# Spreading each cache block's running maximum over the partitions: a transpose of a zero-step column in place of an fp32 product

## The chip, the cores and the metric

The kernel runs on one core of one Trainium2 chip. The metric is the device time of one launch in microseconds (us); lower is better. The same program was run three times, and one more execution was taken with the hardware profiler.

## What is computed

One inference step (one layer) of a hybrid decoder, for a prompt of 1024 tokens and for 8 sequences of 8 sampled tokens each. A combined input projection feeds gated linear attention (GLA) and multi-head latent attention (MLA); an output projection, a gated MLP with a short convolution and a gated per-layer embedding follow. The change lies in the MLA of the sampled tokens. They attend to a paged cache of 8192 latents per sequence, page by page, with a running maximum:

```python
def body(carry, phys):                       # one page of 128 cached latents
    c, r = pool_ckv[phys], pool_krope[phys]
    k, v = latent_to_kv(c, r, w_kvup, g_kn)
    return combine(carry, block_stats(q, k, v, None)), None

# block_stats: s = q.k * scale; m = max(s); p = exp(s - m); l = sum(p); acc = p.v
# combine:     m = max(m1, m2), and both l and acc rescaled by exp(m1 - m), exp(m2 - m)
```

Any shift of the scores that is the same in numerator and denominator gives the same output.

## The kernel before

**The cache stream.** The 8192 cached positions of each of the 8 sequences are worked through in 8 blocks of 1024 positions, 64 blocks in all; the first block of a sequence also takes the 8 new tokens. A block passes through a pipeline written as a generator, `cache_stream`: `stage_load` gathers the pages, `pre`/`turn` transpose the latents (L522, tile `ctp`), `main` forms key sizes and raw scores (L139 to L141, tile `ks`, and ScalarE's squares, tile `csq`), `stage_b` makes the scores `sn` and each column's maximum over the tiles, `stage_c1` makes the running maximum and the exponentials, and `stage_pv` multiplies them with the latents (L645, tile `cpv`).

**The place of the change** is `stage_c1`. The 64 score columns are 8 heads by 8 tokens, and the partition axis holds positions. L616 transposes the column maxima `ml` (128 partitions by 128, each column twice), so that partition c of `mt` holds the maxima of column c; L620 or L622 on VectorE reduces them, together with the old maximum `mo`, to `m` (tile `bm`, 128 partitions by 1). L626 must subtract `m` from scores whose columns lie along the free axis, so `m` has to be turned from a column into a row that stands alike in all 128 partitions. L625 does that on TensorE: it reads `m[0:64]` with a step of zero 128 times (`broadcast_to([64, P])`) as the stationary operand and multiplies it with a 64 x 64 identity in fp32. L628 (exponential), L629 and L630 (the split of the result in two fp32r parts `phl`) follow.

**What sets the order.** Two generators are interleaved while the program is built: the cache stream and `dense`, which holds the prompt's projections, GLA and prompt attention; `PACE` says how much estimated dense work goes with a cache step. After `dense` ends, `fill` and `place` put units of the output projection (`wo_unit`, L1432 to L1436, tile `ps_dn`) between the remaining cache blocks. Within that, the framework's scheduler orders the instructions of each engine by estimated times of its own, so a different instruction at one place can move others, on every engine. Each engine then works its list in order, and a wait of its first instruction holds everything behind it. SP issues most loads and stores as a list of the same kind; its stores wait for the engine that makes the data, its loads for a free staging buffer (three of them, tag `stage`).

Names in the rows below: `ps_pj`, `ps_kv`, `ps_gv`, `ps_lt` are sums of prompt projections; `stage` the staging buffers for weights (`w_in`, `mla_w_qup`, `mla_w_kvup`); `lat` the prompt's latents, stored as `ckv_p` and `krope_p`; `wraw` the raw rows of the output projection's weights `w_o`; `h_...` the residual rows loaded from `x_prompt`; `pt_ol` (L675) the transpose of one sequence's finished output, 64 partitions high.

Of the kernel before, what the change touches and what calls it, by code (L numbers as in the profile page):

```python
# [18 lines left out]
P = 128  # L19
# [25 lines left out]
def step_kernel(ctx: ExitStack, tc: tile.TileContext, A):  # L45
    nc = tc.nc
    pe, act, dve, pool, sp = nc.tensor, nc.scalar, nc.vector, nc.gpsimd, nc.sync
# [4 lines left out]
    def ctile(shape, dt, name):  # L52
        return const.tile(shape, dt, name=name, tag=name)
# [3 lines left out]
    ident = ctile([P, P], F32, "ident")  # L57
# [134 lines left out]
    def pm(shape, name):  # L192
        return psM.tile(shape, F32, tag="m", name=name)
# [412 lines left out]
    def stage_c1(o):  # L606

        nt = o.nt
        sb = o.sn[:, :nt, :]
        mt = pm([P, 512], "mt")  # L610
        drain = o.n - NB * 8 + 3
        if drain == 1:
            fill(49 - z["units"])
        elif drain == 2:
            fill(2)
        pe.transpose(mt[:, 0:P], o.ml.rearrange("p a c -> p (a c)"), ident)  # L616
        m = cp.tile([P, 1], F32, tag="bm", name="bm", bufs=4)
        mo = state.get(o.b)
        if mo is None:
            dve.tensor_reduce(m, mt[:, 0:P], AX.X, ALU.max)  # L620
        else:
            dve.tensor_scalar(mt[:, 256:256 + P], mt[:, 0:P], mo, None, ALU.max, ALU.max, accum_out=m)  # L622
        if drain > 0:
            fill(1)
        pe.matmul(mt[:, P:P + 64], m[0:64].broadcast_to([64, P]), ident[0:64, 0:64], start=True, stop=True)  # L625
        dve.tensor_tensor(sb, sb, mt[:, P:P + 64].unsqueeze(1).broadcast_to([P, nt, 64]), ALU.subtract)  # L626
        phl = cp.tile([P, 9, P], F32R, tag="phl", name="phl", bufs=1)
        act.activation(sb, sb, AF.Exp)  # L628
        act.copy(phl[:, :nt, 0:64], sb)  # L629
        pool.tensor_tensor(phl[:, :nt, 64:128], sb, phl[:, :nt, 0:64].bitcast(F32), ALU.subtract)  # L630
        o.phl = phl
        o.t = None
        if mo is not None:
            o.t = cp.tile([P, 1], F32, tag="mb", name="mb", bufs=4)
            act.activation(o.t, m, AF.Exp, bias=mo, scale=-1.0)
        state[o.b] = m
# [41 lines left out]
    def cache_stream():  # L678
# [7 lines left out]
        for n in range(N + 2):  # L686
            z["block"] = n
            if n + 2 < N:
                blk[n + 2] = stage_load(*todo[n + 2], n + 2)
            if n < N:  # L690
                pre(blk, blk[n], 4)
                main(blk[n], 0)
            if 0 <= n - 2:
                stage_pv(blk[n - 2])
            if 0 <= n - 1 < N:
                stage_b(blk[n - 1])
            yield
            if n < N:
                if blk[n].nt == 9:
                    pre(blk, blk[n], 8)  # L700
                    main(blk[n], 4)
                    pre(blk, blk[n + 1], 0)
                    main(blk[n], 8)
                else:
                    if n + 1 < N:
                        pre(blk, blk[n + 1], 0)
                    main(blk[n], 4)
            if 0 <= n - 1 < N:
                stage_c1(blk[n - 1])
            if 0 <= n - 2:  # L710
                stage_c2(blk.pop(n - 2))
            yield
# [882 lines left out]
    def fill(n):  # L1595
        for _ in range(n):
            z["units"] += next(z["fill"], done) is None
# [658 lines left out]
```

## Time and profile before

| | |
|---|---|
| median of three runs | 2220.92 us (2215.85 to 2221.26) |
| the profiled execution | 2221.39 us, of which the span from first to last instruction is 2219.6 us |
| TensorE (PE) busy | 2134.6 us, 96% of the span |
| VectorE (DVE), ScalarE (ACT), GpSimd (POOL) busy | 1666.6, 1369.1 and 1227.5 us |
| mean granted TensorE clock | 0.984 |
| L625 | first at 116.8 us, last at 1326.0 us, 64 blocks |
| after the cache stream | from about 1330 us: MLP, embedding |

In rows of instructions the columns are: start in us, length in us, engine, line, operation, output tile and inputs, shape, count, and in brackets how long the engine was idle before it and who released it. Lengths of matmuls overlap, because they are pipelined: what a matmul costs its neighbours is read from start to start. PEld is the load of a stationary operand. In rows of windows the columns are the stretch, its length, busy time (and count) of PE, PEld, DVE, ACT and POOL, the granted clock, the DMA engines' busy share and GB/s.

### The profile page before, as it was taken

To read this page: it belongs to the slowest core of one execution; us is meant where nothing else is said; L and a number is where in the kernel's file an instruction comes from. 1 tells how busy PE (TensorE), PEld (TensorE's weight loads), DVE (VectorE), ACT (ScalarE), POOL (GpSimd) and SP (SyncE) were. 2 spreads that over 40 slices of the span, in tenths; PEclk is the share of its full clock that TensorE was granted. 3 is DMA by queue.
4 is the path that set the end of the run, shared out by engine and by line. 5 is a ranking of instruction groups with operands and counts; after the bars stand their busy time and mean duration, and the time that the engine had idled before them with its cause. 6 is when DMAs were issued, how large, how long until landed. Compare 5 with 4: busy or idle time off the path is not lost.

```text
span 2219.6 us, 38384 instructions
## 1 busy us (share of the span) xinstructions
PE 2134.6 (96%) x13460; PEld 1934.7 (87%) x13460; DVE 1666.6 (75%) x2551; ACT 1369.1 (62%) x3726; POOL 1227.5 (55%) x1330
## 2 busy tenths in 40 slices
PE   7999999999999999999999987999999999999999
PEld 6888978878888888887788876999999999888899
DVE  4775676467788888887888878888888886887642
ACT  5576766777778888887777766433333433534631
POOL 5675668576777777777445557666656562011100
PEclk9899999999999999999999998999999999999999
DMA  5343234412342222221521212322232325778321
GB/s 181 110 141 110 77 117 157 141 54 69 104 120 60 64 73 61 60 56 46 167 80 57 76 66 96 105 92 95 91 100 91 100 87 190 238 222 237 98 72 41
DMA packets 204418, 233.07 MB, mean 105 GB/s; under 512 B 42422, under 2 KB 146339, under 8 KB 204227
## 3 DMA queue, kind: packets, MB, share of 16 engines
q1 hardware_dynamic: 188259, 179.49, 25.8%
q0 software_dynamic: 14736, 46.67, 7.3%
q10 hardware_dynamic: 1232, 4.46, 0.5%
q8 instruction: 108, 1.77, 0.3%
q14 instruction: 83, 0.68, 0.1%
HBM read 188.00 MB, written 42.52 MB: 104 GB/s over the span
## 4 chain that ended last, share of the span: by engine, by line
PE 80%; DVE 7%; ACT 5%; DMA 4%; POOL 2%; issue 2%; SPq 0%; DVEq 0%; POOLq 0%; ACTq 0%
PE ps_gu L140 7%; PE ps_gu L141 7%; PE ps_gu L139 7%; PE ks L139 5%; PE ks L141 5%; PE ks L140 4%; PE ps_dn L141 3%; PE ps_dn L140 3%; PE ps_dn L139 3%; PE cpv L645 2%; PE ctp L522 2%; PE ps_lt L278 2%; PE ps_pj L139 2%; PE ps_pj L140 1%; PE ps_pj L141 1%
## 5 line engine op out<-in xcount | busy, mean ns | idle before, releaser
L560 ACT ACTIVATE csq<-ks 128x256 f32<-128x256 f32 x1040 | 392.2, 400 | 88.1 <-PE ks L141 78.0
L565 DVE TENSOR_REDUCE css<-csq 128x16 f32<-128x1024 f32 (+1 forms) x264 | 315.8, 1197 | 63.0 <-ACT csq L560 61.9
L115 ACT CAST wh<-st 128x512 fp32r<-128x512 f32 x176 | 108.4, 619 | 188.6 <-PE ps_gu L140 166.0
L139 PE MATMUL ks<-mv0h,cTh 128*128 128x320 f32 (+1 forms) x520 | 171.9, 333 | 6.9 <-ACT csq L560 3.0
L139 PE MATMUL ks<-mv1h,cTh 128*128 128x320 f32 (+1 forms) x520 | 170.4, 329 | 7.6 <-ACT sn L562 3.6
L604 POOL TENSOR_TENSOR chl<-craw,chl 128x1024 fp32r<-128x1024 f32 x64 | 141.8, 2216 | 57.9 <-ACT chl L603 57.2
L140 PE MATMUL ks<-mv1l,cTh 128*128 128x320 f32 (+1 forms) x520 | 154.0, 298 | 0.0
L140 PE MATMUL ks<-mv0l,cTh 128*128 128x320 f32 (+1 forms) x520 | 153.0, 296 | 0.0
L141 PE MATMUL ks<-mv0h,cTl 128*128 128x320 f32 (+1 forms) x520 | 148.6, 298 | 0.9 <-DVE cTl L116 0.8
L141 PE MATMUL ks<-mv1h,cTl 128*128 128x320 f32 (+1 forms) x520 | 148.9, 300 | 0.0
L630 POOL TENSOR_TENSOR phl<-sn,phl 128x512 fp32r<-128x512 f32 (+1 forms) x64 | 84.8, 1326 | 108.2 <-ACT phl L629 107.9
L116 DVE TENSOR_TENSOR wl<-st,wh 128x512 fp32r<-128x512 f32 x132 | 119.0, 903 | 28.5 <-ACT wh L115 28.5
L116 POOL TENSOR_TENSOR wl<-st,wh 128x512 fp32r<-128x512 f32 x44 | 69.4, 1580 | 103.5 <-ACT wh L115 98.2
L141 PE MATMUL ps_dn<-o 128*128 128x512 f32 x308 | 120.2, 390 | 0.0
L140 PE MATMUL ps_dn<-o 128*128 128x512 f32 x308 | 120.1, 390 | 0.1
L116 DVE TENSOR_TENSOR cTl<-ctp,cTh 128x512 fp32r<-128x512 f32 (+1 forms) x136 | 90.1, 663 | 39.4 <-ACT cTh L115 38.4
L139 PEld LDWEIGHTS ks<-mv0h,cTh 128*128 128x128 f32 x520 | 99.1, 191 | 20.7 <-ACT sn L562 7.1
L562 ACT COPY sn<-ks 128x64 f32<-128x64 f32 x520 | 116.8, 225 | 0.0
L139 PEld LDWEIGHTS ks<-mv1h,cTh 128*128 128x128 f32 x520 | 99.6, 191 | 19.7 <-ACT sn L562 7.4
L1317 POOL TENSOR_TENSOR pl<-p,ph 128x512 fp32r<-128x512 f32 (+1 forms) x96 | 97.1, 1016 | 31.7 <-DVE ph L1316 21.5
L139 PE MATMUL ps_dn<-o 128*128 128x512 f32 x308 | 112.1, 390 | 0.0
L139 PE MATMUL ps_gu<-xrh,wh 128*128 128x320 f32 x352 | 108.6, 309 | 1.1 <-ACT xrh L115 1.1
(672 smaller groups left out, 7875.3 us busy)
## 6 DMA issues: line engine op xcount, KB each, us to landing
raw<-ds SPq DMA_DIRECT2D x77, 256.0 KB
raw<-ffn_w_down SPq DMA_DIRECT2D x66, 256.0 KB
stage<-w_in SPq DMA_DIRECT2D x48, 256.0 KB
st<-ffn_w_gate SPq DMA_DIRECT2D x44, 256.0 KB
st<-ffn_w_up SPq DMA_DIRECT2D x44, 256.0 KB
wr<-ffn_w_down SPq DMA_DIRECT2D x44, 256.0 KB
ds<-cv SPq DMA_DIRECT2D x21, 512.0 KB
oraw<-doT SPq DMA_DIRECT2D x16, 256.0 KB
```

The costliest lines, as they stand in the source:

```text
L115: cast = act.copy(hi, src)
L116: res = (lo_eng or dve).tensor_tensor(lo, src, hi.bitcast(F32), ALU.subtract)
L139: pe.matmul(ps, ah, bh, start=first, stop=False)
L140: pe.matmul(ps, ah, bl, start=False, stop=False)
L141: return pe.matmul(ps, al, bh, start=False, stop=last)
L278: pe.matmul(ps, x, w, start=first, stop=last)
L560: act.activation(sq[:, f * 256:f * 256 + 256], ks[:, 0:256], AF.Square)
L562: act.copy(o.sn[:, g0 + i, :], ks[:, 256:320])
L565: dve.tensor_reduce(o.ss[:, g0 + i + 1 - n:g0 + i + 1, :].rearrange("p i h -> p (i h)"), sq2[:, :n].rearrange("p i (h n) -> p (i h) n", n= ...
L604: pool.tensor_tensor(ch[:, c0:c1, 128:256], src, ch[:, c0:c1, 0:128].bitcast(F32), ALU.subtract)
L630: pool.tensor_tensor(phl[:, :nt, 64:128], sb, phl[:, :nt, 0:64].bitcast(F32), ALU.subtract)
L1317: pool.tensor_tensor(pl[:, c0:], p[:, c0:], ph[:, c0:].bitcast(F32), ALU.subtract)
```

## The change

The one fp32 product per block becomes a transpose with the same operands, the same output and the same place in the source: the data as stationary operand, the identity as moving operand, marked as a transpose.

```diff
         if drain > 0:
             fill(1)
-        pe.matmul(mt[:, P:P + 64], m[0:64].broadcast_to([64, P]), ident[0:64, 0:64], start=True, stop=True)
+        pe.transpose(mt[:, P:P + 64], m[0:64].broadcast_to([64, P]), ident[0:64, 0:64])
         dve.tensor_tensor(sb, sb, mt[:, P:P + 64].unsqueeze(1).broadcast_to([P, nt, 64]), ALU.subtract)
```

No instruction is added or removed in the program besides; on each engine the same instructions stand in another order. On TensorE the order is the old one up to the fourth block and again, but for a few rows, from the 54th block on; between these the prompt's work and the cache blocks are interleaved differently. SP's list differs from the 2nd half of the prompt's projections to the first loads of `w_o`. Three places matter below.

SP, at the prompt's second half, about 270 us into the span (`lat`: the prompt's latents; `stage`: weights on their way in). Before:

```order
L864 DMA ckv_p<-lat 128x128
L865 DMA krope_p<-lat 128x32
L157 DMA stage<-mla_w_qup 128x384 x3
L479 DMA newc<-ckvs 8x128
L157 DMA stage<-mla_w_kvup 128x512
L864 DMA ckv_p<-lat 128x128
L157 DMA stage<-mla_w_kvup 128x512
L157 DMA stage<-w_in 128x4x128
```

After:

```order
L864 DMA ckv_p<-lat 128x128
L157 DMA stage<-mla_w_qup 128x384 x2
L865 DMA krope_p<-lat 128x32
L157 DMA stage<-mla_w_qup 128x384
L157 DMA stage<-mla_w_kvup 128x512 x2
L864 DMA ckv_p<-lat 128x128
L157 DMA stage<-w_in 128x4x128
L479 DMA newc<-ckvs 8x128
```

Two loads of `mla_w_qup` moved ahead of a store that waits for the latents, and the load of `w_in` ahead of `newc`, which waits for TensorE.

SP, at the hand-over from prompt attention to the output projection, about 1060 us into the span (`h_...`: residual rows, 512 KB each; `wraw`: the first weights of the output projection):

```order
 L1550 DMA h_14703<-x_prompt 128x1024
 L1550 DMA h_14700<-x_prompt 128x1024
-L1417 DMA wraw<-w_o 128x512
 L1550 DMA h_14702<-x_prompt 128x1024
-L1417 DMA wraw<-w_o 128x512 x2
 L1550 DMA h_14704<-x_prompt 128x1024
+L1417 DMA wraw<-w_o 128x512 x3
 L1550 DMA h_14692<-x_prompt 128x1024
```

The first load of `w_o` moved behind two more residual loads, the second behind one more.

TensorE, the 48th block, shortly after the first unit of the output projection. Before:

```order
L616 MATMUL mt<-ident,ml 128x128
L139 MATMUL ks<-mv0h,cTh 128x256
L140 MATMUL ks<-mv0l,cTh 128x256
L141 MATMUL ks<-mv0h,cTl 128x256
L139 MATMUL ks<-mv0h,cTh 128x320
L140 MATMUL ks<-mv0l,cTh 128x320
L141 MATMUL ks<-mv0h,cTl 128x320
L139 MATMUL ks<-mv0h,cTh 128x256
L140 MATMUL ks<-mv0l,cTh 128x256
L141 MATMUL ks<-mv0h,cTl 128x256
L625 MATMUL mt<-ident,bm 128x64
```

After:

```order
L1435 MATMUL ps_dn<-wdl,sh 128x512
L1436 MATMUL ps_dn<-wdh,sl 128x512
L522 MATMUL ctp<-ident,craw 128x128 x8
L616 MATMUL mt<-ident,ml 128x128
L625 MATMUL mt<-ident,bm 128x64
L1432 MATMUL ps_dn<-wdh,sh 128x512
```

The nine matmuls between the transpose L616 and L625, which waits for VectorE's maximum, are gone from there. At the 10th block (about 350 us) it is the other way: nine matmuls and four transposes stood between the two, and now 26 matmuls and one transpose.

## Prediction

> **What bounds the kernel now.** I read the page first: busy time per engine, then the chain that ended last by engine.
>
> ```profile
> PE 2134.6 (96%) x13460; PEld 1934.7 (87%) x13460; DVE 1666.6 (75%) x2551; ACT 1369.1 (62%) x3726; POOL 1227.5 (55%) x1330
> PE 80%; DVE 7%; ACT 5%; DMA 4%; POOL 2%; issue 2%; SPq 0%; DVEq 0%; POOLq 0%; ACTq 0%
> ```
>
> TensorE (PE) is busy 96% of the span and carries 80% of the chain. So time taken off PE counts nearly in full, unless PE has slack where it is taken. The table of windows says where it has, over the cache stream:
>
> ```profile
> 115.00:400.00 285.00, 270.97 (x1731) 245.79 (x1731) 190.48 (x324) 196.33 (x613) 193.53 (x207) 0.98 0.38 120
> 400.00:700.00 300.00, 289.03 (x2074) 250.10 (x2073) 215.20 (x368) 229.91 (x715) 208.38 (x275) 0.99 0.34 94
> 700.00:1000.00 300.00, 294.66 (x2034) 258.31 (x2033) 250.72 (x409) 262.68 (x786) 221.49 (x222) 1.00 0.22 61
> 1000.00:1330.00 330.00, 311.26 (x1913) 273.35 (x1912) 264.96 (x404) 243.74 (x749) 177.92 (x166) 0.97 0.25 81
> ```
>
> PE is busy 270.97 + 289.03 + 294.66 + 311.26 = 1165.9 of 1215 us, again 96%; it idles 49 us, spread thinly. Then the changed line itself, in the view by source line, and the wait of PE for it, in the table of waits:
>
> ```profile
> L625 PEld LDWEIGHTS mt<-ident,bm x128: 182/185/245, 116.8 to 1325.9; 64*128 64x128 f32 x128
> L625 PE MATMUL mt<-ident,bm x128: 272/272/320, 116.8 to 1326.0; 64*128 64x64 f32 x128
> PE mt L625 <- DVE mt L622: 5.1, 4, 2.6
> ```
>
> There are 128 of them for 64 blocks: the fp32 product runs as two passes, each with its own weight load. In all blocks together PE waits only 5.1 us in front of it, 4 times, at most 2.6 us.
>
> **The direct term.** What a pass costs PE I read from starts in the timeline: a block with the two-pass product, and a single-pass transpose of the same height that the kernel already has (L675, 64 partitions, 64 columns).
>
> ```profile
> 882.02 0.28 PE L140 MATMUL ks<-mv0l,cTh 128*128 128x256 f32 x1
> 882.14 0.27 PE L141 MATMUL ks<-mv0h,cTl 128*128 128x256 f32 x1
> 882.34 0.43 PE L625 MATMUL mt<-ident,bm 64*128 64x64 f32 x2
> 882.70 0.39 PE L1325 MATMUL o<-pl,vo 128*128 128x256 f32 x1
> 1229.32 0.28 PE L141 MATMUL ks<-mv1h,cTl 128*128 128x256 f32 x1
> 1229.53 0.27 PE L675 MATMUL pt_ol<-ident,ol 64*128 64x64 f32 x1
> 1229.73 0.42 PE L139 MATMUL ks<-mv1h,cTh 128*128 128x320 f32 x1
> ```
>
> The two passes last 0.43 us together and one of them 0.27, so the second starts 0.16 us after the first. From the start of L625 to the next matmul it is 882.70 - 882.34 = 0.36 us; from L675, 0.20 us: the same 0.16 less. The matmul ahead holds PE 0.20 us before the one (882.14 to 882.34) and 0.21 before the other, against 0.12 between two ordinary ones (882.02 to 882.14). So the stalls around a 64-high operand stay, and one pass goes: 64 x 0.16 = 10.2 us of PE time. With PE busy 96% there, 9.8 us reach the end.
>
> Bounds for it: the least is nothing, if the scheduler's new order gives it all back (below). The most would be that the new transpose costs as little as the full-height one of the maxima, L616:
>
> ```profile
> 880.15 0.27 PE L616 MATMUL mt<-ident,ml 128*128 128x128 f32 x1
> 880.18 0.48 PE L1278 MATMUL t<-kh,qh 96*128 96x512 f32 x1
> 880.49 0.28 PE L139 MATMUL ks<-mv0h,cTh 128*128 128x256 f32 x1
> 881.30 0.40 PE L1278 MATMUL t<-kh,qh 96*128 96x512 f32 x1
> 881.54 0.23 PE L1280 MATMUL t<-maskq,identb 128*128 128x128 bf16 x1
> ```
>
> L616 and the 512-column matmul behind it take 880.49 - 880.15 = 0.34 us, and such a matmul alone 881.54 - 881.30 = 0.24, so L616 costs 0.10. L625 costs 882.70 - 882.14 - 0.12 = 0.44. The difference, 0.34 us, times 64 would be 22 us. I take 0.16, because the operand stays `m[0:64]`, 64 partitions high, as L675's is.
>
> The Trainium skill, FP8 and Floating Point Precision, TensorE Precision Notes, counts four passes for true fp32; by that three would go, an estimate of 3 x 0.16 x 64 = 31 us. The row with x128 for 64 blocks shows two, and the measurement decides.
>
> VectorE's subtraction L626 also gets its row 0.16 us sooner per block. That lies beside the next blocks' matmuls, and I cost it at nothing.
>
> **The order.** The instructions stay, but each engine's list is new between the 4th and the 54th block. I looked where PE ran dry before, and what stands there now.
>
> *The load of `mla_w_qup`.* From SP's timeline, the chain, PE's timeline and two windows:
>
> ```profile
> 269.22 0.33 SPq L864 DMA_DIRECT2D ckv_p<-lat  x1
> 273.46 0.33 SPq L865 DMA_DIRECT2D krope_p<-lat  x1
> 273.91 1.63 SPq L157 DMA_DIRECT2D stage<-mla_w_qup  x3
> 274.37 4.25 DMA stage<-mla_w_qup
> 281.67 4.50 DMA stage<-w_in
> 286.92 0.80 PE L139 MATMUL ps_pj<-xTh,w 128*128 128x512 f32 x1 [2.41 <-ACT w L115]
> 270.00:290.00 20.00, 16.06 (x88) 13.45 (x87) 13.53 (x26) 12.32 (x39) 9.73 (x9) 0.90 0.51 151
> 290.00:300.00 10.00, 10.00 (x51) 8.83 (x50) 4.21 (x11) 4.34 (x15) 4.70 (x5) 0.86 0.20 55
> ```
>
> The store of `krope_p` held SP until 273.46, the weights behind it started at 273.91, their staging buffers came free late, `w_in` behind them landed at 281.67 + 4.50 = 286.2, and PE stood 2.41 us. The granted clock then fell: 0.90 over 20 us and 0.86 over 10 lose 2.0 + 1.4 = 3.4 us. In the new order two of these loads stand ahead of that store and may start near 269.6, some 4 us sooner. The gain is between 0 (VectorE or ScalarE late instead) and 2.4 + 3.4 = 5.8 us; I take half, 3 us. Next late there would be the store itself, for which nobody on the chip waits soon.
>
> *The 10th block.* PE waited for VectorE's maximum, and the clock fell once more:
>
> ```profile
> 353.63 0.43 PE L625 MATMUL mt<-ident,bm 64*128 64x64 f32 x2 [2.63 <-DVE mt L622]
> 345.00:360.00 15.00, 12.27 (x74) 10.90 (x74) 11.60 (x20) 10.12 (x33) 10.87 (x13) 0.89 0.60 179
> ```
>
> The new order puts twice as many matmuls between L616 and this one. Gain between 0 and 2.63 + 0.11 x 15 = 4.3 us; I take half the wait, 1.3, since VectorE's own list changed too.
>
> *The hand-over to the output projection.* SP's timeline, the chain, PE's timeline, a window and the issue table:
>
> ```profile
> 1059.70 1.98 SPq L1550 DMA_DIRECT2D h<-x_prompt  x4
> 1062.86 0.33 SPq L1417 DMA_DIRECT2D wraw<-w_o  x1
> 1062.86 5.92 DMA wraw<-w_o
> 1069.48 0.49 PE L1432 MATMUL ps_dn<-wdh,sh 128*128 128x512 f32 x1 [2.06 <-ACT wdh L115]
> 1063.00:1066.00 3.00, 2.36 (x14) 2.04 (x15) 2.63 (x4) 3.00 (x14) 0.00 (x0) 1.00 1.02 391
> h<-x_prompt SPq DMA_DIRECT2D x8, 512.0 KB
> ```
>
> The DMA engines are full here (share 1.02, 391 GB/s), and PE waits for `w_o`. Two more transfers of 512 KB (0.524 MB) ahead cost 2 x 0.524 / 0.391 = 2.7 us; the bounds are 0 (if the staging buffer, not the queue, is last) and twice that, with another fall of the clock. I take 2.7.
>
> *The 48th block.* L625 now stands right behind L616, so PE has nothing to do while VectorE takes the maximum. By the waits of the table (5.1 us in 4, at most 2.6) this costs 0 to 2.6; I take their mean, 1.3.
>
> **The sum.** -9.8 - 3 - 1.3 + 2.7 + 1.3 = -10.1 us. Against the profiled execution's own 2221.39 us (0.47 above the median of the runs shown) that is 2211.3, so I predict 2211. The other moved blocks I can't sum from rows; PE idles 49 us over the stream, and I allow a fifth of that, 10 us, either way. A measurement of this kernel can tell about 0.3% (6.7 us) from no change, so "faster" means below 2214.3 and "slower" above 2227.6.
>
> **The rivals.**
>
> *The order gives more than it takes* (0.14). The stall at 287 us and the one at 353 us vanish whole, and the hand-over loses nothing: -9.8 - 5.8 - 4.3 = -19.9, about 2201. For it: both orders point that way. Against: another engine is usually close behind.
>
> *The order eats the pass* (0.18): the blocks between lose about 10 us in new short waits and come out near 2221. For it: over 50 blocks 0.2 us each is enough. Against: the list has as many places that got better as worse.
>
> *Short cover, slower* (0.12). L625 waits at the head of PE's list for L622; all matmuls behind it, prompt work included, wait too. VectorE is busy 250.72 of 300 us from 700 to 1000 us, so a maximum can come 2 us late. If 12 of the moved blocks stand as the 48th does and wait 2 us, that is +24 - 9.8 = +14, 2235; it decides from 8 such blocks on (16.5 / 2). For it: the 48th block. Against: the 10th, and only 5.1 us of such waits before.
>
> *Transposes let the clock fall, slower* (0.03). The granted clock fell after PE ran dry, at 3.4 us a time around 290 us. If a transpose in place of two passes left PE looking idle often enough that 8 of 64 blocks lost this, it would be +27 - 9.8 = +17, 2239; it decides from 5 falls on (16.5 / 3.4). The Trainium skill, TensorE: Matmul & The Clock Gate, Part 4, says that transposes do not count as busy for the clock in the same way. Against it: the clock is 1.00 from 700 to 1000 us although L616 and other transposes run in every block.
>
> *It doesn't do what it says* (0.03): the transpose of a zero-step fp32 column still runs as two passes. Then only the order's -0.3 is left, 2221.
>
> **The numbers.** The forecast (0.50) has its own range 2204 to 2218; four fifths of it, 0.40, lie below 2214.3. Faster: 0.40 + 0.14 = 0.54. Within 0.3%: 0.10 + 0.18 + 0.03 = 0.31. Slower: 0.12 + 0.03 = 0.15. The range 2199 to 2229 takes in the first, second and last rival and leaves out most of the two slow ones.
>
> **What would show it.** Right: 64 instead of 128 matmuls on L625, 0.20 us from its start to the next matmul, no 2.4 us gap at 287 us. Wrong: 128 of them; gaps named L622 ahead of L625 that sum to far more than 5.1 us; `wraw` more than 9 us on the chain; or a mean granted clock below 0.984 with no longer gaps.

## The result

| | before | after |
|---|---|---|
| median of 22 runs | 2219.51 us (2214.98 to 2221.91) | 2222.08 us (2217.95 to 2230.35) |
| ratio after / before | | 1.0015, 95% interval 1.0007 to 1.0023 |
| profiled execution | 2221.39 us | 2218.45 us |

The forecast was 2211, a gain, with a range of 2199 to 2229. The time lies inside that range, but the change is a loss: it costs 0.0015 x 2220 = 3.3 us (1.6 to 5.1). The profiled execution of after lies at the fast end of its runs, so a sum of its rows understates the loss; where a sum matters, the means of all runs below carry it.

The profile after, first the page: busy time and the chain.

```profile
PE 2119.2 (96%) x13396; PEld 1921.6 (87%) x13396; DVE 1669.8 (75%) x2551; ACT 1366.6 (62%) x3726; POOL 1229.0 (55%) x1330
PE 77%; DVE 8%; ACT 5%; POOL 3%; DMA 3%; issue 3%; SPq 0%; POOLq 0%; DVEq 0%; ACTq 0%
```

PE is busy 15.4 us less, with 64 matmuls fewer: the pass went. But PE's share of the chain fell from 80% to 77%, and GpSimd (POOL), DVE and issue time took its place. The groups of L625 in the view by line, and one block in PE's timeline:

```profile
L625 PEld LDWEIGHTS mt<-ident,bm x64: 129/129/179, 116.8 to 1321.9; 64*128 64x128 f32 x64
L625 PE MATMUL mt<-ident,bm x64: 218/266/366, 116.8 to 1321.9; 64*128 64x64 f32 x64
```

```profile
882.60 0.27 PE L625 MATMUL mt<-ident,bm 64*128 64x64 f32 x1
882.80 0.50 PE L1322 MATMUL o<-ph,vo 128*128 128x512 f32 x1
```

One pass per block, and 0.20 us to the next matmul, as forecast. So the operation did what it should, and the time went elsewhere. The windows of the cache stream:

```profile
115.00:400.00 285.00, 272.02 (x1743) 247.79 (x1743) 199.62 (x328) 199.66 (x620) 196.09 (x212) 0.99 0.39 120
400.00:700.00 300.00, 286.20 (x2062) 248.24 (x2060) 218.60 (x367) 227.48 (x714) 209.60 (x273) 0.98 0.33 94
700.00:1000.00 300.00, 291.81 (x2013) 254.41 (x2012) 246.80 (x411) 261.84 (x782) 222.14 (x222) 1.00 0.22 61
1000.00:1330.00 330.00, 305.08 (x1890) 267.69 (x1890) 265.76 (x402) 244.11 (x754) 178.03 (x168) 0.97 0.26 84
```

PE now idles 59.9 of 1215 us, against 49 before. The table of waits names the new ones (us in total, times, longest):

```profile
PE pa L1177 <- POOL kx L1168: 5.9, 1, 5.9
PE o L1325 <- POOL pl L1317: 5.0, 2, 4.0
PE ps_dn L1432 <- ACT wdh L115: 2.9, 1, 2.9
PE mt L625 <- DVE mt L622: 2.3, 2, 1.8
```

The waits at L625 itself fell (5.1 to 2.3 us). Two waits for GpSimd came, of 5.9 and 4.0 us, neither of them at a place that the prediction looked at.

**The first of them, at 446 us.** GpSimd's timeline and PE's. `kx` (L1168) are the products that GLA's matmul L1177 waits for; L490 and L491 split the next sequence's rotary queries in two fp32r parts, on 32 partitions at a time; L473 is the page gather.

```profile
439.68 1.05 POOL L490 CAST qbd1h<-qr 32x64 fp32r<-32x64 f32 x3 [2.57 <-issue]
441.01 0.98 POOL L473 DMA_INDIRECT craw<-cache_ckv,idx  x1 [0.27 <-POOL qbd1h L490]
443.07 0.31 POOL L491 TENSOR_TENSOR qbd1l<-qr,qbd1h 32x64 fp32r<-32x64 f32 x1
445.32 1.06 POOL L491 TENSOR_TENSOR qbd1l<-qr,qbd1h 32x64 fp32r<-32x64 f32 x3 [1.94 <-DMA craw<-cache_ckv,idx]
446.46 1.28 POOL L1168 TENSOR_TENSOR kx<-kx,qk 128x64 f32<-128x64 f32 x3
446.83 0.93 PE L1177 MATMUL pa<-qb,kx 128*32 128x64 f32 x5 [5.85 <-POOL kx L1168]
```

The second to fourth L491 wait until the gather issued just ahead has landed, though they read nothing of it (the program has a wait there). L1168 stands behind them, and PE behind L1168. In before, L1168 stood ahead of those three:

```profile
446.71 0.98 POOL L473 DMA_INDIRECT craw<-cache_ckv,idx  x1 [0.16 <-issue]
447.71 0.33 POOL L491 TENSOR_TENSOR qbd1l<-qr,qbd1h 32x64 fp32r<-32x64 f32 x1
447.99 2.66 POOL L1168 TENSOR_TENSOR kx<-kx,qk 128x64 f32<-128x64 f32 x5
451.38 0.31 POOL L491 TENSOR_TENSOR qbd1l<-qr,qbd1h 32x64 fp32r<-32x64 f32 x1 [0.73 <-DMA craw<-cache_ckv,idx]
```

And the granted clock around it, the window of before first, that of after second:

```profile
430.00:470.00 40.00, 35.74 (x234) 30.42 (x233) 27.98 (x46) 30.99 (x100) 34.04 (x52) 0.96 0.51 133
```

```profile
430.00:470.00 40.00, 32.06 (x191) 26.46 (x189) 21.89 (x39) 26.02 (x82) 28.07 (x43) 0.83 0.40 107
```

Clock 0.83 in place of 0.96 over 40 us is 5.2 us of clock, and PE is busy 3.7 us less. The two must not be added, since the clock is low during part of the wait too (0.50 from 443 to 446 us), where PE has nothing to lose. Two shorter windows of after show that it stays low when PE works again:

```profile
440.00:450.00 10.00, 4.15 (x26) 3.63 (x25) 3.71 (x7) 1.91 (x7) 7.49 (x15) 0.65 0.19 54
450.00:460.00 10.00, 9.90 (x51) 8.35 (x51) 4.96 (x7) 7.91 (x24) 3.97 (x5) 0.67 0.09 27
```

By the second table below, after loses 6.9 us against before between 440 and 480 us.

### The profile page after: what moved, and what is told of

It reads as the page before. It is cut to its first block, busy times and chain, and to the rows that moved or that the text cites. A ratio compares the mean times of both kernels' runs of the same rounds, so it can differ in the third digit from the quotient of the medians.

```text
span 2216.4 us, 38264 instructions
## 1 busy us (share of the span) xinstructions
PE 2119.2 (96%) x13396; PEld 1921.6 (87%) x13396; DVE 1669.8 (75%) x2551; ACT 1366.6 (62%) x3726; POOL 1229.0 (55%) x1330
## 4 chain that ended last, share of the span: by engine, by line
PE 77%; DVE 8%; ACT 5%; POOL 3%; DMA 3%; issue 3%; SPq 0%; POOLq 0%; DVEq 0%; ACTq 0%
PE ps_gu L141 7%; PE ps_gu L140 7%; PE ps_gu L139 7%; PE ks L139 5%; PE ks L140 4%; PE ks L141 4%; PE ps_dn L140 3%; PE ps_dn L141 3%; PE ps_dn L139 3%; PE cpv L645 2%; PE ctp L522 2%; DVE css L565 2%; PE ps_lt L278 2%; PE ps_pj L139 1%; PE ps_pj L140 1%
## 5 line engine op out<-in xcount | busy, mean ns | idle before, releaser
L139 PE MATMUL ks<-mv1h,cTh 128*128 128x320 f32 (+1 forms) x520 | 169.3, 327 | 10.1 <-ACT sn L562 4.8
L592 POOL TENSOR_TENSOR sn<-sn,cy 128x512 f32<-128x512 f32 (+1 forms) x64 | 70.7, 1105 | 82.5 <-DVE cy L590 72.3
L1317 POOL TENSOR_TENSOR pl<-p,ph 128x512 fp32r<-128x512 f32 (+2 forms) x96 | 97.3, 1021 | 26.8 <-DVE ph L1316 17.7
```

Of the source, the lines that this page charges most:

```text
L139: pe.matmul(ps, ah, bh, start=first, stop=False)
L592: pool.tensor_tensor(snv, snv, y[:, :nt].rearrange("p i h -> p (i h)").unsqueeze(2).broadcast_to([P, nt * 8, 8]), ALU.mult)
L1317: pool.tensor_tensor(pl[:, c0:], p[:, c0:], ph[:, c0:].bitcast(F32), ALU.subtract)
```

## The experiments

The theory after the result: the pass is worth about what was forecast, and the scheduler's new order costs more than that, at few places. Rivals: the pass itself is worth little; the transposes cost clock; the loss is spread over 50 blocks. The first tool is to part order and operation: once the scheduler has set the order, the 64 instructions of L625 are rewritten in place, every engine's list staying as it is. All ratios are to before on the same chip; "us" is the ratio's distance from 1, times 2220. Of the expectations printed below, only that of e9 was met by the theory it was meant for; e1 and e3 ended where a theory that gave the pass little had put them, e2, e4, e5 and e8 ended between two theories, e6 just above its second, and e7, e10, e11 and e12 outside all that was expected.

| kernel | median, us | ratio (95%) | us |
|---|---|---|---|
| e1 old order, transposes | 2216.26 | 0.9979 (0.9968 to 0.9989) | -4.7 |
| e2 new order, products | 2228.56 | 1.0042 (1.0028 to 1.0056) | +9.3 |
| e3 full-height transposes, own order | 2216.10 | 0.9981 (0.9970 to 0.9991) | -4.2 |
| e4 full-height transposes, old order | 2207.55 | 0.9951 (0.9938 to 0.9965) | -10.9 |
| e5 new order early, old-like late, transposes | 2219.14 | 0.9994 (0.9983 to 1.0006) | -1.3 |
| e6 old order early, new late, transposes | 2224.58 | 1.0015 (1.0004 to 1.0025) | +3.3 |
| e7 after, casts on VectorE, own order | 2236.73 | 1.0072 (1.0060 to 1.0084) | +16.0 |
| e8 old order, one pass more | 2225.69 | 1.0021 (1.0011 to 1.0031) | +4.7 |
| e9 after, casts later on GpSimd | 2216.73 | 0.9984 (0.9974 to 0.9995) | -3.6 |
| e10 after, `w_o` first on SP | 2226.30 | 1.0028 (1.0018 to 1.0039) | +6.2 |
| e11 both | 2223.13 | 1.0018 (1.0004 to 1.0031) | +4.0 |
| e12 e4 with `w_o` first | 2210.29 | 0.9956 (0.9941 to 0.9972) | -9.8 |

Two readings of my own over these kernels. First, every run has a span and a mean granted clock. Span times clock is what it would have lasted at full clock, the rest is lost to the clock (means over all runs, us; before as run beside e1 to e4, within 0.6 of that beside the others):

| | before | e1 | after | e2 | e3 | e4 | e5 | e6 | e9 | e10 |
|---|---|---|---|---|---|---|---|---|---|---|
| at full clock | 2182.7 | 2176.9 | 2178.5 | 2186.8 | 2178.7 | 2170.9 | 2176.6 | 2184.7 | 2177.8 | 2180.3 |
| lost to the clock | 35.0 | 36.6 | 42.2 | 39.6 | 35.0 | 34.9 | 41.4 | 37.2 | 36.5 | 43.8 |

Second, where in the span a profiled execution gains or loses: each matmul but L625 is weighed with the median start-to-start time of its kind in before, and the time at which the same sum of work is done is compared with before (us later; a negative number is ahead). These are single executions: after and e9 have the same lists up to 440 us and stand 2.8 us apart there, so a level can be off by 3 us. Steps at one place repeat better: from 350 to 400 us after gains 4.8 us and e9 5.2.

| at, us of before | 250 | 300 | 350 | 400 | 440 | 480 | 700 | 1020 | 1080 | end |
|---|---|---|---|---|---|---|---|---|---|---|
| e1 | 1.4 | 1.1 | 1.0 | 1.5 | 1.9 | 2.4 | 0.3 | -1.8 | -3.2 | -3.2 |
| after | -1.1 | -3.9 | 0.1 | -4.7 | -5.4 | 1.5 | -4.4 | -4.6 | 0.0 | -3.2 |
| e6 | -1.0 | -0.9 | -1.0 | -1.1 | -1.4 | -1.3 | -4.7 | -4.2 | 1.3 | 3.5 |
| e9 | -1.0 | -5.9 | -2.2 | -7.4 | -8.2 | -4.3 | -10.4 | -10.6 | -5.8 | -4.2 |

**Order and pass apart: e1 and e2.** e1 takes before's order and makes the 64 products transposes; e2 takes after's order and makes its transposes products.

```diff
+    swap(nc, transpose=True)   # e1, in before; e2: None, in after
     return nc
```

> The transpose in the old order: after the scheduler has ordered the program with the fp32 product, the 64 instructions of L625 are turned into transposes in place, so every engine's list is that of before and only the second pass is gone. Theory A (the pass is worth what its slot on TensorE says, the new order took it back): about 10 us below before, 2209 to 2211, ratio 0.995 to 0.996. Theory B (TensorE has slack in these blocks, other engines' chains absorb the pass): within 4 us of before, 2216 to 2220. Theory C (a transpose costs granted clock): not below before, with a mean granted clock under 0.980.

> The product in the new order: ordered with the transpose, then the 64 instructions of L625 are turned back into fp32 products in place. Every engine's list is that of the changed kernel, with the second pass back. Theory A: the pass comes back on top of an order that is worse by 12 us, so 2230 to 2234 against 2222 for the changed kernel. Theory B: within 4 us of the changed kernel, 2220 to 2226. Theory C: below the changed kernel.

The pass alone gains 4.7 us (2.4 to 7.1), the order alone costs 9.3 (6.2 to 12.4), and the change lies between. With the new order the pass is worth 9.3 - 3.3 = 6.0. So both steps of the sum were off: the pass brought about half of its 10.2 us, and the order cost 8.0 (from e1 to the change) to 9.3 (e2) where I had summed -0.3.

**A taller operand: e3 and e4.** The transpose reads all 128 partitions of `m` against the full identity. In e3 the scheduler makes its own order; in e4 it is put in place in the old one.

```diff
-        pe.transpose(mt[:, P:P + 64], m[0:64].broadcast_to([64, P]), ident[0:64, 0:64])
+        pe.transpose(mt[:, P:2 * P], m.broadcast_to([P, P]), ident)
```

> The transpose at full height: all 128 partitions of m (its upper 64 repeat the lower) against the 128 x 128 identity, 128 output columns of which 64 are read; the scheduler orders it anew. By the slots of L625 (0.44 us) and L616 (0.10 us) it saves 0.34 us a block, 22 us against the product, if the order is neutral. Theory A: 2198 plus or minus 12 for the order. Theory B: 2214 to 2222.

> The full-height transpose in the old order: ordered with the 64-high product, then the 64 instructions are replaced in place by full-height transposes. Theory A: 64 x 0.34 = 22 us less than before, 2196 to 2200, and 11 to 12 us less than the 64-high transpose in the old order, since the stalls around a 64-high operand go too. Theory B: 2214 to 2220. If a full-height operand does not remove the stalls, it equals the 64-high transpose in the old order.

PE's timeline of e4, a block:

```profile
872.45 0.27 PE L141 MATMUL ks<-mv0h,cTl 128*128 128x256 f32 x1
872.56 0.27 PE L625 MATMUL mt<-ident,bm 128*128 128x128 f32 x1
872.59 0.37 PE L1325 MATMUL o<-pl,vo 128*128 128x256 f32 x1
872.79 0.38 PE L522 MATMUL ctp<-ident,craw 128*128 128x128 f32 x2
```

The stalls ahead of and behind the 64-high operand are gone, as the prediction's upper bound assumed. The median time from the matmul ahead of L625 to the one behind it is, in the same order, 596 ns in before, 433 in e1 and 227 in e4 (408 in after, with other neighbours): from before to e4 64 x 0.369 = 23.6 us less. That points to the height and not to the number of columns: L1177, 128 partitions high with 64 columns, takes 223 ns in before in the same measure where nothing waits. The kernel gains 10.9 (7.8 to 13.8), again about half, and is the fastest of all. With an order of its own (e3) it keeps 4.2: the order costs 6.7 here too.

**One pass more: e8.**

```diff
+    # ahead of each of the 64 products: the same operands as one single-pass transpose, overwritten
```

> Old order, the product kept, and one more single-pass 64-high transpose of the same operands right ahead of each of the 64, its result overwritten: one pass more where the first experiment had one less. If a pass counts on the path by its slot of 0.16 us: +10 us, 2229 to 2230. If only the share counts that the first experiment found (3.3 of 10.2 us): +3 us, 2222 to 2224. If stalls that are fixed by other engines swallow a saving but not a cost: over +6 us, above 2226.

```profile
880.72 0.49 PE L625 MATMUL mt<-ident,bm 64*128 64x64 f32 x3
881.14 0.39 PE L1325 MATMUL o<-pl,vo 128*128 128x256 f32 x1
```

The slot grew from 0.36 to only 0.42 us: this pass costs 0.06, not 0.16, or 3.8 us in 64 blocks, and the kernel became 4.7 (2.4 to 6.9) slower. So an added cost counted about in full (the interval allows two thirds to nearly double), while of a saving half was kept. The expectations had taken 0.16 us for any pass; that was wrong.

**Which part of the order: e5 and e6.** While the order is made, the scheduler sees transposes only in the first 20 blocks (e5) or only in the other 44 (e6); then all 64 are made transposes in place.

```diff
-        pe.transpose(mt[:, P:P + 64], ...)
+        (pe.transpose(mt[:, P:P + 64], ...) if o.n < 20 else pe.matmul(mt[:, P:P + 64], ...))   # e6: >= 20
```

> The scheduler is shown a transpose for cache blocks 0 to 19 and a product for blocks 20 to 63; then, with the order fixed, all 64 are run as transposes. So the order is the new one up to about 580 us (with the wait of TensorE for GpSimd at 446 us), and mostly the old one behind that. Theory T1, the new order loses its time at 446 us, where GpSimd's list waits for a page gather and the clock falls: about 2221 to 2223 us, as the changed kernel. Theory T2, it loses it late, between 1020 and 1080 us (the second wait for GpSimd at 1031 us, the hand-over to the output projection): about 2215 to 2217 us, as the old order with transposes (2216.3).

> The reverse: a product shown for blocks 0 to 19, a transpose for blocks 20 to 63, then all 64 run as transposes. The order is the old one up to about 600 us and the new one behind that. T1: 2215 to 2218 us, and no wait of TensorE for GpSimd above 3 us near 446 us. T2: 2221 to 2223 us. If early and late order cost half each: both this and the early one come out near 2219.

Against e1 (-4.7) the early order costs 3.4 and the late one 8.0; together that is more than the 8.0 of the whole order, by no more than the noise of the four kernels. In the expectations T1 is the theory that the new order loses its time at 446 us, T2 that it does so late, at the hand-over. Taken alone this speaks for T2. But the two tables part them: e5 loses to the clock (41.4, like after's 42.2), e6 hardly (37.2); and after and e9 stand 5 to 8 us ahead of before at 440 us, which e6 does not. The early order gains that, and after loses it again within 40 us. T1 and T2 are both right in part, and the gain that I had forecast hides between them. In the late order the loss isn't one wait: between 1020 and 1080 us PE waits 10.6 us for other engines in e6, in nine waits, and 7.0 in e1, in nine; of these only 1.9 and 1.5 us are for `w_o`.

**Taking the wait for the gather away: e7, then e9.** In e7 the casts run on VectorE.

```diff
-            pool.tensor_copy(qb4[0], qv)
-            pool.tensor_tensor(qb4[1], qv, qb4[0].bitcast(F32), ALU.subtract)
+            dve.tensor_copy(qb4[0], qv)
+            dve.tensor_tensor(qb4[1], qv, qb4[0].bitcast(F32), ALU.subtract)
```

> The changed kernel with the two casts of a sequence's rotary queries (L490, L491) on VectorE in place of GpSimd, so that nothing on GpSimd waits there for the page gather that was just issued. The scheduler makes an order of its own again. T1: the wait of 5.85 us at 446 us and the half-clock spell behind it go, and with them 5 to 8 us: 2214 to 2217 us. T2: the late losses stay, 2220 to 2223 us. In both the profile must show no wait of TensorE for L1168 above 2 us; if it does, the gather was not the cause.

The wait at L1168 is gone, but the kernel is 16 us slower, since the scheduler made yet another order, with waits elsewhere. PE's timeline of e7:

```profile
343.05 0.79 PE L139 MATMUL ps_kv<-wkv,lTh 128*128 128x512 f32 x1 [3.28 <-ACT qt L320]
357.99 0.54 PE L141 MATMUL ks<-mv1h,cTl 128*128 128x320 f32 x2 [3.57 <-DVE cTl L116]
```

As a test of the wait it settles nothing: an edit in the source moves everything. e9 therefore moves only the casts, on GpSimd's finished list, with the counts of the waits renumbered; no other engine's list changes.

```diff
 L473 DMA craw<-cache_ckv,idx          # at 446 us
 L592 TENSOR_TENSOR sn<-sn,cy
-L491 TENSOR_TENSOR qbd1l<-qr,qbd1h x4
 L1168 TENSOR_TENSOR kx<-kx,qk x3
 L599 COPY ml<-ml
 L1168 TENSOR_TENSOR kx<-kx,qk x2
+L491 TENSOR_TENSOR qbd1l<-qr,qbd1h x4
...
 L490 CAST qbd1h<-qr                   # at 1031 us
-L490 CAST qbd1h<-qr x3
-L491 TENSOR_TENSOR qbd1l<-qr,qbd1h x4
 L592, L1317, L594
+L490 CAST qbd1h<-qr x3
+L491 TENSOR_TENSOR qbd1l<-qr,qbd1h x4
```

> The changed kernel with its order fixed, but for GpSimd's list at two places: at 446 us the four casts L491 that wait for the page gather just issued stand behind the five products L1168 for which TensorE waits, and at 1031 us seven of the casts L490 and L491 behind L592, one L1317 and L594. The other engines' lists are untouched. T1, these two waits and the clock falls behind them are the early half of what the order costs: the waits of 5.85 us and 3.98 us shrink below 2 us each, and the time falls by 5 to 9 us, to 2213 to 2217 us. Rival, another engine (ScalarE's exponentials for L1168, VectorE) is close behind: 2220 to 2222 us.

GpSimd's and PE's timeline of e9, and its window:

```profile
437.95 0.98 POOL L473 DMA_INDIRECT craw<-cache_ckv,idx  x1 [0.27 <-DVE cy L590]
440.34 1.46 POOL L1168 TENSOR_TENSOR kx<-kx,qk 128x64 f32<-128x64 f32 x3
443.43 1.43 POOL L491 TENSOR_TENSOR qbd1l<-qr,qbd1h 32x64 fp32r<-32x64 f32 x4
440.71 0.41 PE L1177 MATMUL pa<-qb,kx 128*32 128x64 f32 x4 [1.00 <-POOL kx L1168]
```

```profile
430.00:470.00 40.00, 35.53 (x216) 29.83 (x216) 26.35 (x49) 29.22 (x94) 29.71 (x53) 0.91 0.32 94
```

The wait fell from 5.85 to 1.00 us, the clock of the window is 0.91 and not 0.83, and the ratio went from 1.0015 to 0.9984: moving eleven small casts gave back 6.9 us (about 4 to 10 by the two intervals). By the means, 5.7 us of it is time lost to the clock (42.2 to 36.5) and 0.7 work. e9 is faster than before (1.1 to 5.8 us) with the operation of the change.

The size is less sure than that one pair says. e11 has the same edit on top of e10 (both below), and there it gave back 2.2 us (6.2 to 4.0), within the noise of the two. In the profile of e11 PE still waits 2.8 us for L1168, and without the edit, in the same order, it waits 3.0 us in e2 and 5.1 in e10. What the edit takes out of GpSimd's own list is steady: from the start of the gather to that of L1168 it is 5.45 us in after and 2.39 in e9 by the rows above, 3.1 less. The second table has the same at the place: after loses 6.9 us between 440 and 480 us, e9 3.9. At the second place little was won: in place of 3.98 us PE now waits 1.72, 1.68 and 2.68 us for the next in line. PE's timeline, first after, then e9:

```profile
1031.62 0.47 PE L1325 MATMUL o<-pl,vo 128*128 128x128 f32 x1 [3.98 <-POOL pl L1317]
```

```profile
1026.40 1.22 PE L645 MATMUL cpv<-chl,phl 128*128 128x258 f32 x8 [1.72 <-POOL phl L630]
1034.94 0.51 PE L1325 MATMUL o<-pl,vo 128*128 128x512 f32 x1 [1.68 <-POOL pl L1317]
1038.60 0.69 PE L522 MATMUL ctp<-ident,craw 128*128 128x128 f32 x2 [2.68 <-ACT p L1315]
```

So I put the gain down to the first place; the two were not run apart. The second table agrees: e9 is 6.0 us ahead of after at 1020 and 5.8 at 1080 us.

**The hand-over: e10, e11, e12.** In the finished order of SP, two of the three `w_o` loads go ahead of the residual loads; e11 adds e9's edit, e12 does it in e4.

```diff
+L1417 DMA wraw<-w_o 128x512 x2
 L1550 DMA h_...<-x_prompt 128x1024 x6
-L1417 DMA wraw<-w_o 128x512 x3
+L1417 DMA wraw<-w_o 128x512
```

> The changed kernel with its order fixed, but for SP's list at one place: the first two loads of w_o that stood behind six residual loads of 512 KB stand ahead of them. T2, the hand-over loses its time to these transfers: the wait for w_o on TensorE falls from 2.90 us to under 1.5 us, the time by 2 to 4 us, to 2218 to 2220 us. Rival, the staging buffer and not the transfers in flight is last: within 1 us of the changed kernel (2222).

> Both edits together. If the two places are what the new order costs, the time comes to what the old order gives with the same transposes (2216) or below it: 2211 to 2216 us. If the loss is spread over other places: 2218 to 2221 us.

> The best kernel so far (full-height transposes in the old order, 2207.6 us) with its first two remaining loads of w_o ahead of the residual loads. If the transfers in flight hold the hand-over: 2205 to 2206.5 us. If the staging buffer does: 2207 to 2209 us.

PE's wait for `w_o` in after and in e10, one row each, and the pieces of e10's chain behind it:

```profile
1069.77 0.80 PE L1432 MATMUL ps_dn<-wdh,sh 128*128 128x512 f32 x1 [2.90 <-ACT wdh L115]
```

```profile
1068.29 0.80 PE L1432 MATMUL ps_dn<-wdh,sh 128*128 128x512 f32 x1 [2.61 <-ACT wdh L115]
```

```profile
1062.12 10.03 DMA h<-x_prompt
1072.92 8.04 DMA oraw<-doT
```

The wait shrank by 0.3 us, and the kernel became slower (1.0028 against 1.0015; e11 against e9: 1.0018 against 0.9984). With `w_o` ahead, the residual rows stand on the chain, and behind them `oraw`, rows of the attention output for the same product. The DMA engines are full in both cases (share 1.02 in after and 1.00 in e10 from 1060 to 1080 us), and another transfer is last. That this is what makes e10 slower isn't shown: by the weighing of the second table it loses 4.6 us between 1060 and 1080 us where after loses 3.2, and most of the rest only behind 1100 us. e12 does not beat e4 either. The tables of waits between 1030 and 1090 us, of e4 and then of e12:

```profile
PE ps_dn L1432 <- ACT wdh L115: 2.3, 1, 2.3
PE ks L139 <- ACT sn L562: 0.3, 1, 0.3
```

```profile
PE ks L139 <- ACT sn L562: 4.7, 2, 4.4
```

The wait for `w_o` is gone, and a longer one for ScalarE's scores has come. In e11 e9's gain is lost again.

## Why the prediction was wrong, point by point

- **The pass.** One pass instead of two, slot 0.36 to 0.20 us: right. "9.8 us reach the end": wrong, 4.7 (e1) to 6.0. The share of busy time, 96%, is not the share of a saving that is kept. In e1's profile nothing is kept up to 480 us (2.4 us behind, 1.6 of these by the start of its first block) and 5.6 between there and 1080. What takes the other half stays open. It isn't longer waiting in e1: there PE idles 85.9 us of the span and in before 85.0. A part is clock: over all runs 36.6 us lost against 35.0.
- **The bounds.** The upper bound, 22 us for a full-height operand, was right as PE time (23.6 by the rows) and double in effect (10.9).
- **The load of `mla_w_qup` and the 10th block.** Right, and too small: after is 2.8 us further ahead at 300 than at 250 us, and 4.8 further at 400 than at 350. The gap of 2.63 us is gone; that of 2.41 us has become 1.78 and 0.96, with the clock at 0.97 from 250 to 300 us where before had 0.93. Between the two stretches it loses 4.0, to waits that I did not look for. PE's timeline of after:

```profile
280.16 0.41 PE L139 MATMUL ks<-mv1h,cTh 128*128 128x320 f32 x1 [1.78 <-ACT csq L560]
282.61 0.79 PE L139 MATMUL ps_pj<-xTh,w 128*128 128x512 f32 x1 [0.96 <-ACT lTh L115]
317.47 0.50 PE L139 MATMUL ps_pj<-xTh,w 128*128 128x512 f32 x1 [1.73 <-ACT sqk L940]
333.38 0.55 PE L909 MATMUL pt_cq<-ident,lat 128*128 128x128 f32 x3 [1.82 <-ACT qt L320]
335.82 0.41 PE L139 MATMUL ks<-mv1h,cTh 128*128 128x320 f32 x1 [1.89 <-ACT cTh L115]
```

- **"The other moved blocks I can't sum": this is the step that failed.** I summed the order to -0.3 from four places where before had a stall, and put the rest at nothing with 10 us either way. The order costs 8.0 us (e1 to the change, 0.9979 to 1.0015), because it makes stalls where there was none, and the clock falls behind them: by the means 5.6 us more is lost to the clock than in e1 (42.2 against 36.6), and 1.6 otherwise. Of the 13.4 us between the forecast -10.1 and the measured +3.3, 8.3 are the order and 5.1 the pass. One such stall, GpSimd's casts between the gather and L1168, costs 2.2 us (e11 against e10) to 6.9 (e9 against after). It is not the whole: e6 has the old order there, without that wait, and is as slow as the change. The move of L1168 behind L491 stood in GpSimd's new list, and the length of a gather in the trace of before; I read SP's and PE's lists for the places with a wait, and not GpSimd's.
- **The hand-over.** `wraw` took 9.20 us on the chain where 5.92 stood before, past the 9 us that I had named as a sign of wrong, and after loses 4.6 us between 1020 and 1080 us (forecast: 2.7 + 1.3). The remedy for the cause that I gave wins nothing: with `w_o` ahead of the loads the wait shrinks or goes, and another takes its place (e10, e12). What of the late order costs e6 its 8.0 us stays open, but for this. At the 48th block PE waits 0.51 us at L625, not 1.3.
- **The rivals.** "The order eats the pass" came nearest, by stalls at a few places and not by 0.2 us a block. Short cover of L625 did not happen (2.3 us in 2). The clock did fall, by 7.2 us of lost time, but not for the transposes: with them in place e1, e3 and e4 lose 34.9 to 36.6, before 35.0. No run here shows the rule of the Trainium skill (TensorE: Matmul & The Clock Gate, Part 4) that transposes do not count as busy for the clock in the same way; 64 of 13,396 matmuls are a weak test of it.

## What to carry to other kernels

With a scheduler, an edit is two edits: the operation and the order. Price them apart by putting the operation into the old order; and in a new list look for new neighbours on every engine, above all for whatever now stands between a transfer just issued and an instruction that the busiest engine waits for. Here about half of what was saved on an engine that is 96% busy was kept, in e1 and in e4: don't count on the whole before a run says so. And a stall can cost more than its length, through the clock: in after 6.9 us between 440 and 480 us, with 5.85 us of wait.

## What the hardware showed that I had not expected

- A 64-high operand is what made L625 dear: in the same order 596 ns from neighbour to neighbour with two passes, 433 with one, 227 for one full-height pass with twice the rows and columns.
- A single-pass transpose of the same operands ahead of the product's two passes adds 0.06 us (e8); the second pass of the product adds 0.16.
- One stall can bring the clock down behind it: with 5.85 us without matmuls the clock of the ten busy microseconds behind is 0.67 (after, 450 to 460 us), and the mean over 40 us 0.83; with a wait of 1.00 us in its place that mean is 0.91 (e9).
